# Query heads of an encoder layer turned two at a time, with the high and low parts of odd heads in exchanged rows

## The chip, the cores and the metric

The kernel runs on one core of a Trainium2 chip. A core has engines with queues of their own: PE (TensorE, matrix products; its weight loads are shown as PEld), DVE (VectorE), ACT (ScalarE), POOL (GpSimd) and SP (SyncE, which here only issues DMAs). Each works through its queue in order, and an instruction waits until the semaphores that it names have come. The metric is the time of one execution on the device in microseconds. A profile records one execution.

## The reference

One layer of a bidirectional encoder on two sequences of 512 tokens, width 1024: an RMS norm, one input projection, a window attention and a state-space branch, both gated and added, an output projection, and a squared-ReLU MLP. What matters here is the attention, with 16 query heads and 4 key heads of 64 channels, in blocks of 128 tokens:

```python
def windowed_attention(q, k, v, sink, bias, mask):
    ...
        s = jnp.einsum('nqkgd,njkd->nkgqj', qb, kw).astype(jnp.float32) * scale + bias
        s = jnp.where(mask[:, None, None], s, NEG_INF)
        sink_col = jnp.broadcast_to(sink_b, s.shape[:-1] + (1,))
        p = jax.nn.softmax(jnp.concatenate([s, sink_col], axis=-1), axis=-1)[..., :-1]
        o = jnp.einsum('nkgqj,njkd->nqkgd', p.astype(vs.dtype), vw)
...
    q = rms_norm(q.reshape(bsz, seq_len, N_HEADS, HEAD_DIM), q_gain)
    k = rms_norm(k.reshape(bsz, seq_len, N_KV_HEADS, HEAD_DIM), k_gain)
```

Each query block of 128 tokens sees its own block of keys and the two beside it.

## The kernel before

Every fp32 product is made of parts in the type fp32r: a high part (a rounded copy, written by ACT) and a low part (the rest, written by DVE). A product of two such operands takes three matmuls: high by high, high by low and low by high.

The program has these stages: norm and turn of x, input projections beside the state-space branch, a short stretch that projects the values and the first query tiles (up to about 459 us), the attention loop (to about 695 us), the gates and the output projection, and the MLP.

The attention loop goes over eight steps, one for each pair of key head `j` and sequence `sq`, and in each over four query blocks `qb`. The text calls one pass a unit, so a step is units 0 to 3. Units 0 and 3 have two key blocks (256 keys), units 1 and 2 three (384 keys). A unit works on three things at once, in an order written out by hand (lines 979 to 1073), which PE, ACT, DVE and POOL keep as it stands:

- `cur`, the unit itself: `scores` (L823, PE), `largest` (L827, DVE, adds the bias and takes the row's largest), `exp` (L833, ACT).
- `prev`, the unit before: `turn` (L839, PE, transposes the probabilities), `high` (L843, ACT), `low` (L848, DVE), `value` (L855, PE, product with the values), `lower_part` (L859, ACT) and `add` (L865, DVE).
- the query tile for the next step (class `Tile`): `project` (L772, PE), `square` (L778, ACT), `power` (L782, DVE, and two POOL instructions), `norm` (L789, DVE), and then, one unit later, `turn` (L794, PE), `high` (L799, ACT) and `low` (L802, DVE).

A step also turns the next keys in unit 0 (L754 on PE, L755 on ACT, L756 on DVE), and in unit 1 it sends its row sums to DRAM and fetches the factor `fac`, by which DVE multiplies the step before in unit 3 (L893). Weight pieces come in between (L730 on ACT, L731 on DVE).

The score product has 128 rows of contraction. For one head, the query operand `qa` holds the 64 channels of the high part in rows 0 to 63 and those of the low part in rows 64 to 127. The keys are copied twice before they are turned, so `kh` has the high part of the same 64 channels in both halves of its rows, and `kl` the low part. Two matmuls with `kh` and `kl` then give all four products of parts.

The changed methods have 32 tiles to work on: three before the loop (their `turn`, `high` and `low` stand among the products of the values), four in each of steps 0 to 6 and one in step 7. In unit 0 the tile belongs to the step itself, in the others to the next.

Of the kernel before, what the change touches and what calls it, by code (L numbers as in the profile page):

```python
# [12 lines left out]
F32 = mybir.dt.float32  # L13
F32R = mybir.dt.float32r
I32 = mybir.dt.int32
AF = mybir.ActivationFunctionType
ALU = mybir.AluOpType
AX = mybir.AxisListType

P = 128  # L20
# [7 lines left out]
CB = 256  # L28
N_HEADS = 16
N_KV = 4  # L30
G = 4
# [32 lines left out]
def hybrid_layer(ctx, tc, x, rel, onehot, w_qkv, w_ug, vectors, lam, coefs, w_glu, w_out, ln2,  # L64
                 w_up, w_down, out):
    nc = tc.nc
    V, S, PE, GP, SP = nc.vector, nc.scalar, nc.tensor, nc.gpsimd, nc.sync
# [12 lines left out]
    def acc():  # L80
        return ps_acc.tile([P, 512], F32, tag="acc", name="acc")
# [22 lines left out]
    ident = const.tile([P, P], F32, name="ident")  # L104
# [5 lines left out]
    bglu_sb, gain_q, gain_k, nsink = [vec[:, a:b] for a, b in ((0, 8), (8, 9), (9, 10), (10, 26))]  # L110
# [331 lines left out]
    with tc.tile_pool(name="hst", bufs=1) as hp:  # L442
        h = hp.tile([P, NCHUNK, 2, GROUPS, NSEQ], F32, name="h")
# [251 lines left out]
    with tc.tile_pool(name="att", bufs=2, reuse_waits="tile") as ap, tc.tile_pool(name="attc", bufs=1, reuse_waits="tile") as ac:  # L695
# [18 lines left out]
        weights, keys, queries, biases = {}, {}, {}, {}  # L714
# [44 lines left out]
        class Tile:  # L759
# [30 lines left out]

            def turn(self):
                self.pt = self.pt or acc()
                for h in range(G):
                    PE.transpose(self.pt[0:64, h * P:(h + 1) * P], self.qn[:, h], ident)  # L794

            def high(self):
                self.ptv = self.pt[0:64].rearrange("p (h t) -> p h t", h=G)
                self.dst = queries[self.key][:, :, self.t * P:(self.t + 1) * P]
                S.activation(self.dst[0:64], self.ptv, AF.Copy, scale=gain_q[0:64])  # L799

            def low(self):
                V.scalar_tensor_tensor(self.dst[64:128], self.ptv, gain_q[0:64], self.dst[0:64].bitcast(F32),  # L802
                                       op0=ALU.mult, op1=ALU.subtract)

        class Unit:

# [133 lines left out]
        rows = None  # L940
        for t in range(4):
# [9 lines left out]
            rows = new  # L951
# [21 lines left out]
        with tc.manual_schedule(engines={ET.PE, ET.Activation, ET.DVE, ET.Pool}):  # L973
            for i, (j, sq) in enumerate(steps):
# [4 lines left out]
                for qb in range(NB):  # L979
                    if 1 <= i < 5:  # L980
                        e, t = divmod((i - 1) * NB + qb, T)
# [89 lines left out]
                    owed, prev, rows = prev, cur, new  # L1071
# [36 lines left out]
    with tc.tile_pool(name="glu", bufs=1, reuse_waits="tile") as gpool, \  # L1108
# [40 lines left out]
        for u in range(2 * KT):  # L1149
            m, s = divmod(u, 2)  # L1150
# [151 lines left out]
    with tc.tile_pool(name="up", bufs=2, reuse_waits="tile") as fp:  # L1302
        turn = itertools.count()

        def parts(src):
            i = next(turn) % KT
            hi, lo = [q[:, i, :].rearrange("p (k n) -> p k n", k=4) for q in ring]
            S.copy(hi, src)  # L1308
            V.tensor_sub(lo, src, hi.bitcast(F32))  # L1309
            return hi, lo  # L1310
# [239 lines left out]
```

## Time and profile before

| what | value |
| --- | --- |
| runs shown | 1509.11, 1509.28, 1507.25 us; median 1509.11 |
| the profiled execution | 1509.57 us, of which the span of recorded work is 1507.8 us |
| granted TensorE clock, mean over the span | 0.993 |
| DMA, mean over the span | 166 GB/s |
| DVE busy in `low` of the query tiles (L802) | 23.8 us in 32 instructions |
| ACT busy in `high` of the query tiles (L799) | 21.5 us in 32 instructions |
| PE matmuls of the turns (L794) | 128 |

A line of the time line has the start in us from the span's start, the duration in us, engine, line and operation, what is written and read, the shape, and a count; in brackets stands how long the engine was idle before it and what ended that. Several PE instructions in a row are merged, and their matmuls overlap each other. A line of the groups has the count, then the busy time in us and the mean of one in ns, then the idle time before.

### The profile page before, as it was taken

What the parts mean: (1) busy time and instruction counts of PE and PEld (TensorE: products, weight loads), DVE (VectorE), ACT (ScalarE), POOL (GpSimd) and SP (SyncE); (2) the same over time, 40 slices, a digit from 0 to 9 for tenths busy, and PEclk for the clock granted to TensorE, in tenths of its full rate; (3) what the DMA queues carried; (4) which work ended last, traced back from release to release, by engine and by line L of the source; (5) the groups of instructions that cost most, each with busy time, mean ns of one, the idle gap of its engine ahead of it and who ended that gap; (6) DMA issues with size and microseconds to landing.
All of it is one profiled execution on the core that took longest, in us unless ns stands there. A gap on an engine that the chain in (4) does not pass through costs nothing. (4 is left out here: it accounts for less than half of the span.)

```text
span 1507.8 us, 22144 instructions
## 1 busy us (share of the span) xinstructions
PE 1452.1 (96%) x8074; PEld 1232.2 (82%) x8074; DVE 1116.3 (74%) x2015; ACT 763.4 (51%) x1362; POOL 192.4 (13%) x362
## 2 busy tenths in 40 slices
PE   6999999999999999997999989999999999999998
PEld 4788888888999998985787878888888888888787
DVE  7998859986647998886985478777777588575653
ACT  6777852235436787783343255544555443433332
POOL 3143341002232332220100000000000000000000
PEclk9999999999999999998999999999999999999999
DMA  4454469239731444373644234444443694454431
GB/s 173 140 168 168 164 211 344 98 111 352 279 103 36 149 138 142 111 257 110 224 164 170 94 103 173 154 153 154 154 154 126 251 361 135 154 181 154 126 122 61
DMA packets 102141, 249.69 MB, mean 166 GB/s; under 512 B 12266, under 2 KB 23786, under 8 KB 102032
## 3 DMA queue, kind: packets, MB, share of 16 engines
q1 hardware_dynamic: 58352, 135.88, 27.6%
q0 software_dynamic: 18048, 57.72, 11.1%
q10 hardware_dynamic: 25632, 54.67, 9.7%
q8 instruction: 64, 1.05, 0.3%
q14 instruction: 45, 0.37, 0.1%
HBM read 173.74 MB, written 90.21 MB: 175 GB/s over the span
## 5 line engine op out<-in xcount | busy, mean ns | idle before, releaser
L185 PE MATMUL acc<-act,c_hi 128*128 128x512 f32 x768 | 249.8, 400 | 1.0 <-DVE act L304 1.0
L117 PE MATMUL bank<-b_lo,a_hi 128*128 128x512 f32 x448 | 174.6, 390 | 1.3 <-DVE b_lo L1419 1.1
L118 PE MATMUL bank<-b_hi,a_lo 128*128 128x512 f32 x448 | 174.3, 389 | 0.0
L116 PE MATMUL bank<-b_hi,a_hi 128*128 128x512 f32 x448 | 173.5, 389 | 0.0
L185 PEld LDWEIGHTS acc<-act,c_hi 128*128 128x128 f32 x768 | 142.2, 189 | 29.2 <-DVE act L304 2.4
L185 PE MATMUL acc<-act,c_lo 128*128 128x512 f32 x384 | 152.5, 397 | 0.0
L1418 ACT CAST a_hi<-d_a 128x1024 fp32r<-128x1024 f32 x56 | 59.1, 1054 | 179.5 <-PE bank L117 176.1
L116 PE MATMUL bank<-act,act 128*128 128x512 f32 x368 | 144.3, 392 | 4.9 <-ACT act L1308 4.9
L117 PE MATMUL bank<-act,act 128*128 128x512 f32 x368 | 144.0, 391 | 0.0
L118 PE MATMUL bank<-act,act 128*128 128x512 f32 x368 | 143.9, 391 | 0.0
L1419 DVE TENSOR_TENSOR a_lo<-d_a,a_hi 128x1024 fp32r<-128x1024 f32 x56 | 68.5, 1223 | 100.0 <-ACT a_hi L1418 100.0
L772 PE MATMUL acc<-w_hi,act 128*128 128x256 f32 x512 | 116.1, 295 | 0.0
L117 PEld LDWEIGHTS bank<-b_lo,a_hi 128*128 128x128 f32 x448 | 84.1, 188 | 19.6 <-DVE b_lo L1419 2.3
L116 PEld LDWEIGHTS bank<-b_hi,a_hi 128*128 128x128 f32 x448 | 84.1, 188 | 17.6
L118 PEld LDWEIGHTS bank<-b_hi,a_lo 128*128 128x128 f32 x448 | 84.1, 188 | 17.4
L123 PE MATMUL acc<-act,gc_hi 128*128 128x512 f32 x256 | 83.9, 407 | 13.7 <-ACT ga L1133 10.7
L772 PEld LDWEIGHTS acc<-w_hi,act 128*128 128x128 f32 x512 | 86.9, 189 | 3.7
L116 PEld LDWEIGHTS bank<-act,act 128*128 128x128 f32 x368 | 69.6, 189 | 19.8 <-ACT act L1308 5.3
L185 PEld LDWEIGHTS acc<-act,c_lo 128*128 128x128 f32 x384 | 72.6, 189 | 13.8 <-DVE c_lo L176 0.5
L833 ACT ACTIVATE p<-p,nmx 128x257 f32<-128x257 f32 (+1 forms) x128 | 72.2, 564 | 22.7 <-DVE nmx L827 21.1
L118 PEld LDWEIGHTS bank<-act,act 128*128 128x128 f32 x368 | 69.6, 189 | 14.8 <-DVE act L1309 0.4
L117 PEld LDWEIGHTS bank<-act,act 128*128 128x128 f32 x368 | 69.6, 189 | 14.4
(328 smaller groups left out, 3426.5 us busy)
## 6 DMA issues: line engine op xcount, KB each, us to landing
d_a<-a_scr SPq DMA_DIRECT2D x56, 512.0 KB, 3.6
u_raw<-in_w_up_dram SPq DMA_DIRECT2D x32, 512.0 KB, 5.1
a_scr<-t ACTq DMA_DIRECT2D x64, 256.0 KB, 5.0
k<-in_w_down_dram SPq DMA_DIRECT2D x32, 512.0 KB, 6.0
c_raw<-in_w_ug_dram SPq DMA_DIRECT2D x48, 256.0 KB, 3.8
a_scr<-a ACTq DMA_DIRECT2D x46, 256.0 KB, 2.1
ct_scr<-ctab POOLq DMA_DIRECT2D x16, 576.0 KB, 3.9
ctab_in<-ct_scr POOLq DMA_DIRECT2D x16, 576.0 KB, 7.8
```

The costliest lines, as they stand in the source:

```text
L116: PE.matmul(ps, a[0], b[0], start=first, stop=False)
L117: PE.matmul(ps, a[0], b[1], start=False, stop=False)
L118: PE.matmul(ps, a[1], b[0], start=False, stop=last)
L123: PE.matmul(ps, w[wi][:, k, :], rows[yi], start=k + p == 0, stop=k == KT - 1 and p == 2)
L185: PE.matmul(ps, w[wi][:, k, :], hT[s][hi][:, k, :], start=n == 0, stop=n == 3 * KT - 1)
L772: PE.matmul(self.ps, hT[sq][act][:, k, col:col + P], w[:, k % 4, :], start=i == 0, stop=i == 3 * KT - 1)
L833: S.activation(p, p, AF.Exp, bias=self.nmx[:, h:h + 1], scale=-1.0, accum_out=self.sums[:, h, self.qb:self.qb + 1])
L1418: S.copy(hi, src)
L1419: V.tensor_sub(lo, src, hi.bitcast(F32))
```

## The change

In the four heads of a tile the first and third are even (e = 0), the second and fourth odd (e = 1). Before, each head was turned by itself: a 128x64 block becomes 64 rows of 128 tokens. Now two neighbouring heads are turned together: a 128x128 block becomes 128 rows, with the even head in rows 0 to 63 and the odd one in rows 64 to 127. Even heads keep their layout in `qa`. For odd heads the high part is written to rows 64 to 127, where it was turned to, and the low part to rows 0 to 63. As both halves of the key operands hold the same channels, the scores are the same sums.

`high` and `low` each work on one parity at a time, so each becomes two instructions of 64 rows and 256 columns where there was one of 64 rows and 512.

```diff
             def turn(self):
                 self.pt = self.pt or acc()
-                for h in range(G):
-                    PE.transpose(self.pt[0:64, h * P:(h + 1) * P], self.qn[:, h], ident)
+                for m in range(2):
+                    PE.transpose(self.pt[:, m * P:(m + 1) * P],
+                                 self.qn[:, 2 * m:2 * m + 2].rearrange("p e d -> p (e d)"), ident)
 
             def high(self):
-                self.ptv = self.pt[0:64].rearrange("p (h t) -> p h t", h=G)
-                self.dst = queries[self.key][:, :, self.t * P:(self.t + 1) * P]
-                S.activation(self.dst[0:64], self.ptv, AF.Copy, scale=gain_q[0:64])
+                self.ptv = self.pt[:, 0:CB].rearrange("p (m t) -> p m t", m=2)
+                self.dst = [queries[self.key][:, e::2, self.t * P:(self.t + 1) * P] for e in range(2)]
+                for dst, rows in zip(self.dst, (slice(0, 64), slice(64, 128))):
+                    S.activation(dst[rows], self.ptv[rows], AF.Copy, scale=gain_q[rows])
 
             def low(self):
-                V.scalar_tensor_tensor(self.dst[64:128], self.ptv, gain_q[0:64], self.dst[0:64].bitcast(F32),
-                                       op0=ALU.mult, op1=ALU.subtract)
+                for dst, rows, other in zip(self.dst, (slice(0, 64), slice(64, 128)), (slice(64, 128), slice(0, 64))):
+                    V.scalar_tensor_tensor(dst[other], self.ptv[rows], gain_q[rows], dst[rows].bitcast(F32),
+                                           op0=ALU.mult, op1=ALU.subtract)
```

On PE nothing but the turn changes. This is its first place, in the stretch before the loop, with the rows of before and of the change; `act` are the turned tokens, `qn` is the normed query tile, and `ident` the identity matrix.

```order
 L772 MATMUL acc<-w_lo,act_103 128x256
 L772 MATMUL acc<-w_hi,act_104 128x256
-L794 MATMUL acc<-ident,qn 64x128 x4
+L794 MATMUL acc<-ident,qn 128x128 x2
 L116 MATMUL acc<-w_hi,act_103 128x256
 L117 MATMUL acc<-w_lo,act_103 128x256
```

Four transposes with 64 output rows became two with 128, at the same place.

On DVE this is unit 3 of step 2 before, with the semaphores that each instruction waits for; `p` are the scores, `nmx` the row's largest, `tps` and `ph` the turned probabilities and their high part, `pl` their low part.

```order
L848 TENSOR_TENSOR pl<-tps,ph 128x512 [waits DVE_49,Activation_49]
L827 ISA p,nmx<-sps,bias,vec 128x256 [waits PE_49]
L827 ISA nmx 128x1
L802 SCALAR_TENSOR_TENSOR qa<-acc,vec,qa 64x4x128 [waits Activation_49]
L848 TENSOR_TENSOR pl<-tps,ph 128x512 [waits DVE_49,Activation_49]
L782 TENSOR_REDUCE ms<-sq 128x4 [waits Activation_49]
```

And the same place now, where three source lines more shift the numbers (L830 was L827, L851 was L848, L805 was L802):

```order
L851 TENSOR_TENSOR pl<-tps,ph 128x512 [waits DVE_49,Activation_49]
L830 ISA p,nmx<-sps,bias,vec 128x256 [waits PE_49]
L830 ISA nmx 128x1
L805 SCALAR_TENSOR_TENSOR qa<-acc,vec,qa 64x2x128 [waits PE_49,Activation_49]
L805 SCALAR_TENSOR_TENSOR qa<-acc,vec,qa 64x2x128
L851 TENSOR_TENSOR pl<-tps,ph 128x512 [waits DVE_49,Activation_49]
L782 TENSOR_REDUCE ms<-sq 128x4 [waits Activation_49]
```

The low part became two instructions, one behind the other; only the first has waits, on ACT and on PE.

On ACT, unit 3 of step 2 before; `vec` holds the gain, `ol` is the lower half of the value product.

```order
L833 ACTIVATE p,sm<-p,nmx 128x257 [waits DVE_49]
L799 ACTIVATE qa<-acc,vec 64x4x128 [waits PE_49]
L843 CAST ph<-tps 128x512 [waits PE_49,Activation_49]
L833 ACTIVATE p,sm<-p,nmx 128x257 [waits DVE_49]
L778 ACTIVATE sq<-acc 128x256 [waits PE_49]
```

And now (L836 was L833, L801 was L799, L846 was L843):

```order
L836 ACTIVATE p,sm<-p,nmx 128x257 [waits DVE_49]
L801 ACTIVATE qa<-acc,vec 64x2x128 [waits PE_49]
L801 ACTIVATE qa<-acc,vec 64x2x128
L846 CAST ph<-tps 128x512 [waits PE_49,Activation_49]
L836 ACTIVATE p,sm<-p,nmx 128x257 [waits DVE_49]
L778 ACTIVATE sq<-acc 128x256 [waits PE_49]
```

The high part became two instructions in a row, the second without a wait. Apart from the three steps of the tile the order on PE, ACT, DVE and POOL is the same. On SP one load of weights and one store of row sums change places in step 7.

## The prediction

> **What bounds the kernel now.** First the busy time of each engine, over the span and by stage.
>
> ```profile
> PE 1452.1 (96%) x8074; PEld 1232.2 (82%) x8074; DVE 1116.3 (74%) x2015; ACT 763.4 (51%) x1362; POOL 192.4 (13%) x362
> ...
> core 0: us, PE busy (x) PEld busy (x) DVE busy (x) ACT busy (x) POOL busy (x), PEclk, DMA share, GB/s
> 433.00:455.00 22.00, 22.00 (x187) 22.00 (x186) 6.85 (x14) 4.86 (x11) 4.50 (x8) 1.00 0.00 1
> 516.00:545.00 29.00, 28.03 (x209) 25.90 (x207) 26.23 (x67) 22.65 (x58) 9.71 (x17) 1.00 0.45 135
> ```
>
> PE leads the whole span, but the changed lines run only between 432 and 668 us, so the stage counts. In its first part (433 to 455 us) PE is busy all the time and DVE a third of it. In the attention loop (516 to 545 us is one step of four units, about 29 us) PE has 28.0 us, but DVE has 26.2 us too. The share does not say which of them sets the pace. The waits between 459 and 672 us and the time lines do.
>
> ```profile
> PEld po L855 <- DVE pl L848: 8.7, 20, 0.8
> ...
> 533.23 0.60 PE L794 MATMUL acc<-ident,qn 128*64 128x128 f32 x4
> 533.67 0.60 PE L839 MATMUL tps<-ident,p 128*128 128x128 f32 x4
> 536.91 0.50 PE L855 MATMUL po<-pl,va 128*128 128x512 f32 x1 [0.51 <-DVE pl L848]
> ...
> 521.44 0.75 DVE L756 SCALAR_TENSOR_TENSOR kl<-tps,vec,kh 128x512 fp32r<-128x512 f32 x1 [0.97 <-ACT kh L755]
> 522.22 0.74 DVE L802 SCALAR_TENSOR_TENSOR qa<-acc,vec,qa 64x512 fp32r<-64x512 f32 x1
> 523.09 0.42 DVE L782 TENSOR_REDUCE ms<-sq 128x4 f32<-128x256 f32 x1
> 529.79 0.42 DVE L782 TENSOR_REDUCE ms<-sq 128x4 f32<-128x256 f32 x1 [0.27 <-ACT sq L778]
> 534.15 0.68 DVE L848 TENSOR_TENSOR pl<-tps,ph 128x512 fp32r<-128x512 f32 x1
> 534.75 0.61 DVE L827 CUSTOM_DVE_ANT_0 p<-sps,bias,vec 128x384 f32<-128x384 f32 x1
> 535.39 0.74 DVE L802 SCALAR_TENSOR_TENSOR qa<-acc,vec,qa 64x512 fp32r<-64x512 f32 x1
> 536.17 0.69 DVE L848 TENSOR_TENSOR pl<-tps,ph 128x512 fp32r<-128x512 f32 x1
> 537.69 0.49 DVE L827 CUSTOM_DVE_ANT_0 p<-sps,bias,vec 128x256 f32<-128x256 f32 x1 [0.51 <-PE sps L823]
> 538.43 1.23 DVE L893 TENSOR_TENSOR ya<-ya,fac 128x1024 f32<-128x1024 f32 x1 [0.25 <-DMA fac<-rs_scr]
> 543.52 0.74 DVE L802 SCALAR_TENSOR_TENSOR qa<-acc,vec,qa 64x512 fp32r<-64x512 f32 x1 [0.24 <-ACT qa L799]
> 544.29 0.69 DVE L848 TENSOR_TENSOR pl<-tps,ph 128x512 fp32r<-128x512 f32 x1
> ...
> 520.71 0.69 ACT L755 ACTIVATE kh<-tps,vec 128x512 fp32r<-128x512 f32 x1 [0.61 <-PE tps L754]
> 521.30 0.67 ACT L799 ACTIVATE qa<-acc,vec 64x512 fp32r<-64x512 f32 x1
> 528.78 0.62 ACT L833 ACTIVATE p<-p,nmx 128x385 f32<-128x385 f32 x1 [0.30 <-DVE nmx L827]
> 542.31 0.51 ACT L833 ACTIVATE p<-p,nmx 128x257 f32<-128x257 f32 x1 [0.26 <-DVE nmx L827]
> 542.82 0.67 ACT L799 ACTIVATE qa<-acc,vec 64x512 fp32r<-64x512 f32 x1
> 543.39 0.57 ACT L843 CAST ph<-tps 128x512 fp32r<-128x512 f32 x1
> ```
>
> These are PE, DVE and ACT of step 2. The pace passes from engine to engine. Unit 0 runs at PE's pace: DVE waits 0.97 us at L756 for a chain that PE's key transposes release. In unit 1 DVE works on without a break from 523.09, and its one idle stretch, 0.27 us, stands behind the query step at 529.79. In unit 2 the last L848 of DVE (536.17) lies behind the query's L802 (535.39), and PE stands until it ends. In unit 3 the chain is L833, L799 on ACT, then L802 and L848 on DVE. So an instruction on DVE or ACT beside the query step is on the path in units 2 and 3, and one that PE saves is on it in unit 0 alone.
>
> Whether the end of the loop reaches the end of the program is seen behind it:
>
> ```profile
> 681.84 1.22 DVE L893 TENSOR_TENSOR ya<-ya,fac 128x1024 f32<-128x1024 f32 x1
> ...
> 702.10 1.23 DVE L893 TENSOR_TENSOR ya<-ya,fac 128x1024 f32<-128x1024 f32 x1 [6.95 <-DMA fac<-rs_scr]
> ```
>
> The last factor (702.10) comes back from DRAM after 6.95 us of waiting and all that follows hangs on it, so I take the rest as moved whole. The factor before it (681.84) is not waited for.
>
> **The change, part by part.** Prices first.
>
> ```profile
> L794 PE MATMUL acc<-ident,qn 128*64 128x128 f32 x128 | 19.3, 273 | 0.0
> L799 ACT ACTIVATE qa<-acc,vec 64x512 fp32r<-64x512 f32 x32 | 21.5, 673 | 0.8 <-PE acc L794 0.5
> L802 DVE SCALAR_TENSOR_TENSOR qa<-acc,vec,qa 64x512 fp32r<-64x512 f32 x32 | 23.8, 744 | 3.3 <-ACT qa L799 2.5
> L843 ACT CAST ph<-tps 128x512 fp32r<-128x512 f32 x80 | 46.1, 576 | 6.8 <-PE tps L839 6.2
> L710 ACT CAST va<-acc 128x256 fp32r<-128x256 f32 x8 | 3.0, 373 | 20.6 <-PE acc L118 20.6
> L848 DVE TENSOR_TENSOR pl<-tps,ph 128x512 fp32r<-128x512 f32 x80 | 54.9, 686 | 2.1 <-ACT ph L843 1.6
> L789 DVE TENSOR_TENSOR qn<-acc,rq 128x256 f32<-128x256 f32 x32 | 13.3, 414 | 5.9 <-POOL rq L785 5.9
> L335 DVE SCALAR_TENSOR_TENSOR ex_q<-ex_q,ex_r 128x64 f32<-128x64 f32 x10 | 2.3, 226 | 0.2
> ```
>
> PE, per tile of 32: four L794 hold the stream from 533.23 to 533.67, 0.11 each. Four L839, which load 128 columns where L794 loads 64, read 0.60 in the time line too, so a wider one should cost the same. Two fewer give **-0.22 us**; the other end is 0, if a transpose twice as wide took twice as long.
>
> ACT, per tile: one 64x512 becomes two 64x256. From L843 to L710, 256 columns fewer save 0.203 us, so a half is 0.673 - 0.203 = 0.47. The next ACT instruction starts 0.10 before the old one's end (543.39 against 542.82 + 0.67), so the pair ends after 0.37 + 0.47 = 0.84 where the one took 0.67: a = **+0.17 us**. Ends: 0 (only the columns count) and +0.27 (no overlap).
>
> DVE, per tile: one 64x512 becomes two 64x256. By L848 and L789 a half saves 0.272, giving 0.744 - 0.272 = 0.47; by L335, the same operation at 64 columns, (0.744 - 0.226) / 448 gives 0.45. The next instruction starts 0.03 to 0.04 after L802's end (536.17 against 536.13). The pair so takes 2 x 0.505 = 1.01 where the one took 0.78: d = **+0.23 us**. The upper end is +0.37, if a half saved only ACT's 0.203; the lower is +0.12, if a half let its successor in 0.08 early, as L848 does (534.75 against 534.15 + 0.68) and L802 does not. I take 0.23 because L802's own rows show no overlap.
>
> The Trainium skill, "VectorE: DVE Perf Modes", section "Two Vector instructions with no wait between them", holds an instruction back until the earlier ones have finished when its start quadrant of input or output differs from that used last; L802 reads the lower rows and writes the upper ones, and the trace agrees with its gap of 0.03 us. The second half then reads and writes the other way round, so both are held and d = 0.23; without the rule d would be 0.12.
>
> The wait between them: in the changed order the first DVE half waits for ACT and the second waits for nothing, though it reads what the second ACT half wrote. So the first waits for both ACT halves; the two pairs do not run side by side. Behind DVE's pair stand the next L848 and PE's last value product; behind ACT's pair the next L843 or L833. DMA queues, POOL and SP get nothing from the tile steps; one store and one load on SP change places in step 7, ahead of the factor at 681.84, and as DVE does not wait for that one I count nothing.
>
> The sum, with d = 0.23, a = 0.17.
> - Before the loop: three tiles, PE alone busy: 3 x -0.22 = -0.66.
> - Unit 0, steps 1 to 6: L756 starts 0.22 earlier at 521.22 and DVE is free 0.78 + 0.78 + 0.23 later, at 523.01 instead of L782's 523.09. ACT's pair ends at 521.08 + 0.84 = 521.92 and is covered. -0.08 each, -0.48.
> - Unit 1: L802 stretches by 0.23 into the 0.27 us before L782; ACT's L833 waits 0.30 for DVE, which covers a. 0. If that cover went, d would count here too, 1.4 us in six steps.
> - Unit 2: DVE is unbroken, d counts whole. Steps 1, 3, 6: 3 x 0.23. Steps 2 and 4 wait for the factor straight behind it (0.25 and 0.66), which covers d: 0. In step 5 L802 waits for ACT itself: a + d = 0.40. Together 1.09.
>
> ```profile
> 597.38 1.23 DVE L893 TENSOR_TENSOR ya<-ya,fac 128x1024 f32<-128x1024 f32 x1 [0.66 <-DMA fac<-rs_scr]
> 623.28 0.75 DVE L802 SCALAR_TENSOR_TENSOR qa<-acc,vec,qa 64x512 fp32r<-64x512 f32 x1 [0.21 <-ACT qa L799]
> 484.93 0.74 DVE L802 SCALAR_TENSOR_TENSOR qa<-acc,vec,qa 64x512 fp32r<-64x512 f32 x1
> 668.55 0.62 DVE L827 CUSTOM_DVE_ANT_0 p<-sps,bias,vec 128x384 f32<-128x384 f32 x1 [0.74 <-PE sps L823]
> ```
>
> - Unit 3, steps 1 to 6: the chain from 542.31 goes through both pairs: a + d = 0.40 each, 2.40.
> - Step 0: -0.22 (PE's pace at first), +0.23 in unit 2, and in unit 3 (484.93, no idle time before it) d with little of a, 0.28: +0.29.
> - Step 7 has one tile, and DVE waits for PE behind it (668.55): -0.22.
>
> The sum is -0.66 - 0.48 + 1.09 + 2.40 + 0.29 - 0.22 = **+2.4 us**. The profiled execution took 1509.57 (its span 1507.8 and 1.8 around it) and would take 1512.0; the median of the three runs is 1509.11, 0.5 lower, so the forecast is **1511.5**. With the lower ends (a = 0, d = 0.12) the same walk gives -0.8, with the upper ones +6.5.
>
> **The rivals.** 0.2% is 3.0 us, about what a measurement of this kernel can tell from no change.
> - PE sets the pace everywhere. For it: 28 of 29 us busy. Against it: DVE's waits for PE are short, and PE's waits at L855 stand in all steps. It would give 32 x -0.22 = -7.0: 1502.1.
> - The pairs cost more than their rows say. Place: unit 3, ACT to DVE, and unit 2. At d = 0.30 and a = 0.20 the walk gives +4.2: 1513.3. It decides from d = 0.26 on, a half of 0.52 us with its gap. For it: no row has this operation at 64x256. Against it: three slopes put the half at 0.45 to 0.47.
> - The first DVE half starts behind the first ACT half. In unit 3 it would start at 543.32, and L848 at 544.33 instead of 544.29: 0.04 in place of 0.40. The sum is about -0.2: 1509.0. Against it: the order of waits. The Trainium skill, "PSUM — Partial Sum Buffer", section "PSUM bank collisions raise a hardware error", has two engines collide only in one bank and one quadrant, and the halves read different ones, so by it nothing forbids this; no run here shows it.
> - The change does not save on PE, because a wider transpose takes 0.22: the terms -0.66, -0.22 (twice) go, and unit 0 adds 0.14 six times in place of its gain: +4.8, 1513.9. Against it: L839's 0.60.
>
> **How the numbers follow.** Chances: my walk 0.51 (of which 0.08 come out over +3.0), dearer pairs 0.27, halves side by side 0.10, PE everywhere 0.07, no saving 0.05. Faster by over 0.2%: 0.07. Slower: 0.08 + 0.27 + 0.05 = 0.40. Within: 0.43 + 0.10 = 0.53. The range goes from the lower ends (1509.11 - 0.8, and 0.3 for the spread of the runs), 1508.0, to 1515.0; it leaves out the PE rival and the top of the dear pairs.
>
> **What would show it.** In the changed profile: PE turns at 0.22 for two; ACT halves near 0.47, the second 0.37 behind the first; DVE halves near 0.47, 0.50 apart, the first never before the second ACT half ends; DVE's wait for ACT in unit 3 up from 0.24 to about 0.4; L782's 0.27 in unit 1 nearly gone; PE's waits at L855 longer. Steps 1 to 6 would each be 0.3 to 0.7 us longer, most at 0.55. Wrong would be: DVE halves over 0.50, a first half that starts early, or waits at L855 that vanish.

## The result, and the profile after it

The changed kernel takes 1516.69 us (median of 4 runs, 1515.52 to 1517.74) and the kernel before 1509.19 us (4 runs, 1507.25 to 1510.24). The ratio is 1.0051, with a 95% interval from 1.0037 to 1.0065: the change makes the kernel 5.6 to 9.8 us slower. The forecast was 2.4 us slower, with a range that ended at 1515.0. The direction was right, the size too small by a factor of three. The two profiled executions (1515.52 and 1509.57 us) differ by 5.95 us, less than the medians (7.5), so what is read from the profiles below explains these 5.95 us; the other 1.5 is not seen in them, and the runs of one kernel spread by 2 to 3 us.

Besides the lines named above, L858 was L855, L885 was L882 (a small copy on ACT) and L896 was L893. The page of the changed kernel (profiled execution 1515.52 us) says:

```profile
span 1513.4 us, 22103 instructions
...
PE 1450.7 (96%) x8010; PEld 1226.0 (81%) x8010; DVE 1123.6 (74%) x2047; ACT 773.6 (51%) x1394; POOL 192.1 (13%) x362
```

PE has 1.4 us less work, DVE 7.3 us and ACT 10.2 us more, and the span is 5.6 us longer. So PE stands still for 7.0 us more than before. The waits between 459 and 677 us say for what (us in total, times, longest):

```profile
PEld po L858 <- DVE pl L851: 16.9, 25, 1.1
...
PE po L858 <- DVE pl L851: 9.3, 14, 0.8
...
DVE qa L805 <- ACT qa L801: 4.8, 10, 0.6
...
DVE ms L782 <- ACT sq L778: 1.4, 7, 0.4
```

For DVE's low part of the weights the weight loads waited 8.7 us before and wait 16.9 now. DVE itself waits more for ACT's high part of the queries (2.5 before), and less at L782 (5.5 before), where it now comes later itself.

The two lines of the query step, all 64 instructions of each (min, median, max in ns; first and last start):

```profile
L801 ACT ACTIVATE qa<-acc,vec x64: 452/468/473, 432.2 to 672.0; 64x256 fp32r<-64x256 f32 x64
...
L805 DVE SCALAR_TENSOR_TENSOR qa<-acc,vec,qa x64: 476/483/490, 434.7 to 673.0; 64x256 fp32r<-64x256 f32 x64
```

A half takes 0.468 and 0.483 us, near the 0.47 that three slopes had given. The durations were not the error. The time line of step 2 shows what stands between the instructions. First the kernel before, in rows that were not shown yet:

```profile
528.13 0.60 DVE L827 CUSTOM_DVE_ANT_0 p<-sps,bias,vec 128x384 f32<-128x384 f32 x1
...
530.12 0.61 DVE L827 CUSTOM_DVE_ANT_0 p<-sps,bias,vec 128x384 f32<-128x384 f32 x1
...
529.30 0.19 ACT L833 ACTIVATION_READ_ACCUMULATOR p<-p,nmx 128x1 f32 x1
529.39 0.36 ACT L778 ACTIVATE sq<-acc 128x256 f32<-128x256 f32 x1
...
523.42 0.61 DVE L827 CUSTOM_DVE_ANT_0 p<-sps,bias,vec 128x384 f32<-128x384 f32 x1
```

And the same step of the changed kernel, DVE, then ACT:

```profile
521.68 0.75 DVE L756 SCALAR_TENSOR_TENSOR kl<-tps,vec,kh 128x512 fp32r<-128x512 f32 x1 [0.76 <-ACT kh L755]
522.52 0.98 DVE L805 SCALAR_TENSOR_TENSOR qa<-acc,vec,qa 64x256 fp32r<-64x256 f32 x2
523.55 0.42 DVE L782 TENSOR_REDUCE ms<-sq 128x4 f32<-128x256 f32 x1
524.01 0.62 DVE L830 CUSTOM_DVE_ANT_0 p<-sps,bias,vec 128x384 f32<-128x384 f32 x1
...
528.72 0.61 DVE L830 CUSTOM_DVE_ANT_0 p<-sps,bias,vec 128x384 f32<-128x384 f32 x1
...
530.52 0.42 DVE L782 TENSOR_REDUCE ms<-sq 128x4 f32<-128x256 f32 x1 [0.17 <-ACT sq L778]
530.97 0.62 DVE L830 CUSTOM_DVE_ANT_0 p<-sps,bias,vec 128x384 f32<-128x384 f32 x1
...
536.25 0.98 DVE L805 SCALAR_TENSOR_TENSOR qa<-acc,vec,qa 64x256 fp32r<-64x256 f32 x2
537.27 0.69 DVE L851 TENSOR_TENSOR pl<-tps,ph 128x512 fp32r<-128x512 f32 x1
...
544.55 0.98 DVE L805 SCALAR_TENSOR_TENSOR qa<-acc,vec,qa 64x256 fp32r<-64x256 f32 x2 [0.51 <-ACT qa L801]
...
528.24 0.24 ACT L885 COPY row<-tps 16x128 f32<-16x128 f32 x1
528.39 0.94 ACT L801 ACTIVATE qa<-acc,vec 64x256 fp32r<-64x256 f32 x2
529.37 0.62 ACT L836 ACTIVATE p<-p,nmx 128x385 f32<-128x385 f32 x1
529.89 0.19 ACT L836 ACTIVATION_READ_ACCUMULATOR p<-p,nmx 128x1 f32 x1
530.10 0.38 ACT L778 ACTIVATE sq<-acc 128x256 f32<-128x256 f32 x1
...
543.58 0.94 ACT L801 ACTIVATE qa<-acc,vec 64x256 fp32r<-64x256 f32 x2
544.54 0.59 ACT L846 CAST ph<-tps 128x512 fp32r<-128x512 f32 x1
```

Three things are to be seen.

- **DVE's pair** takes 0.98 and its successor starts 0.03 behind it (536.25 to 537.27: 1.02 where L802 to L848 was 0.78). That is d = 0.24.
- **ACT's pair** takes 0.94: its halves do not overlap, and the next ACT instruction starts 0.96 behind the pair's start (543.58 to 544.54), where it was 0.57 (542.82 to 543.39). DVE, which started 0.70 behind L799 in unit 3, starts 0.97 behind L801 (544.55). So a = 0.27 for DVE, and 0.39 for ACT's next instruction. DVE's first half waits for both ACT halves, though they read different rows.
- **Instructions behind the pairs, which the change does not touch,** start later than they did. L830 starts 0.46 and 0.45 behind L782 (523.55 to 524.01, 530.52 to 530.97), where it was 0.33. ACT's `sq` starts 0.21 behind the accumulator's read (529.89 to 530.10), where it was 0.09.

To see where the steps grew, take PE's last value product (L855, now L858) in units 2 and 3 of each step as marks in both time lines. Between the marks the loop grew by (us; the forecast's terms beside it):

| step | units 0 to 2, forecast | measured | unit 3, forecast | measured |
|---|---|---|---|---|
| 1 | 0.15 | 0.63 | 0.40 | 0.49 |
| 2 | -0.08 | 0.63 | 0.40 | 0.17 |
| 3 | 0.15 | 0.64 | 0.40 | 0.50 |
| 4 | -0.08 | 0.63 | 0.40 | -0.26 |
| 5 | 0.32 | 1.00 | 0.40 | 0.50 |
| 6 | 0.15 | 0.63 | 0.40 | 0.51 |
| sum | 0.61 | 4.16 | 2.40 | 1.91 |

In steps 2 and 4 the wait for the factor takes something back. The forecast had put that into unit 2; the factor stands behind PE's mark, so the measurement shows it in unit 3. The growth reaches the end whole. This is the last factor in the time line of the changed kernel, 5.40 us later than before:

```profile
707.50 1.23 DVE L896 TENSOR_TENSOR ya<-ya,fac 128x1024 f32<-128x1024 f32 x1 [7.18 <-DMA fac<-rs_scr]
```

### The profile page after: what moved, and what is told of

Read it like the earlier page. It is cut to its first block, busy times and chain, and to the rows that moved or that the text cites. A ratio compares the mean times of both kernels' runs of the same rounds, so it can differ in the third digit from the quotient of the medians.

```text
span 1513.4 us, 22103 instructions
## 1 busy us (share of the span) xinstructions
PE 1450.7 (96%) x8010; PEld 1226.0 (81%) x8010; DVE 1123.6 (74%) x2047; ACT 773.6 (51%) x1394; POOL 192.1 (13%) x362
## 4 chain that ended last, share of the span: by engine, by line
PE 76%; DVE 9%; issue 5%; ACT 4%; DMA 3%; POOL 1%; ACTq 0%; SPq 0%; DVEq 0%; POOLq 0%
PE acc L185 14%; PE bank L118 13%; PE bank L117 13%; PE bank L116 13%; PE acc L123 5%; PE acc L117 2%; PE acc L118 2%; PE acc L116 2%; DVE pl L851 2%; PE acc L772 2%; PE sps L547 2%; PE po L858 1%; PE sps L826 1%; DVE p L830 1%; DVE ya L868 1%
## 5 line engine op out<-in xcount | busy, mean ns | idle before, releaser
L836 ACT ACTIVATE p<-p,nmx 128x257 f32<-128x257 f32 (+1 forms) x128 | 72.3, 565 | 22.5 <-DVE nmx L830 21.1
```

Of the source, the lines that this page charges most:

```text
L836: S.activation(p, p, AF.Exp, bias=self.nmx[:, h:h + 1], scale=-1.0, accum_out=self.sums[:, h, self.qb:self.qb + 1])
```

## The experiments

Two theories were set against each other. **H**: the costs come from the exchange of rows, because an instruction that starts in other rows of PSUM than the one before it on its engine is held until that one has ended; this makes the pairs longer and holds what stands behind them. **S**: the costs come from splitting one instruction into two. A time below is the difference that the ratio gives, times 1509; its 95% interval stands behind it. The change itself is counted by its medians, 7.5 (its ratio gives 7.7).

### One part of the change alone

The turn alone, with one instruction each on ACT and DVE (the edit of `turn` is that of the change):

```diff
...
 def high(self):
-    self.ptv = self.pt[0:64].rearrange("p (h t) -> p h t", h=G)
-    self.dst = queries[...]
+    pt = self.pt[0:64, 0:CB].rearrange("p (m t) -> p m t", m=2)
+    self.ptv = pt[:, None].to_broadcast([64, 2, 2, P])
+    self.dst = queries[...].rearrange("p (e m) t -> p e m t", e=2)
     S.activation(self.dst[0:64], self.ptv, AF.Copy, scale=gain_q[0:64])
```

> The two wide turns of the change, with one ACT and one DVE instruction per tile as before, both reading the lower 64 rows. Heads 0 and 2 of a tile stand in for all four (heads 0, 1, 2, 3 get the queries of 0, 2, 0, 2), so the scores of the others are not computed from their own queries. Theory 1 (PE saves 0.22 us a tile, but it is on the path only before the loop and in unit 0): about -2.6 us against the kernel before. Rival (PE sets the pace everywhere): -7. Rival (a wide turn saves nothing): 0.

Measured: -2.7 us (-4.4 to -1.1). So the turn saves what the forecast had it save, and PE does not set the pace everywhere.

The split alone, with the rows and turns of before:

```diff
-S.activation(self.dst[0:64], self.ptv, ...)
+for hs in (slice(0, 2), slice(2, 4)):
+    S.activation(self.dst[0:64, hs], self.ptv[:, hs], ...)
...
-V.scalar_tensor_tensor(self.dst[64:128], self.ptv, ...)
+for hs in (slice(0, 2), slice(2, 4)):
+    V.scalar_tensor_tensor(self.dst[64:128, hs], self.ptv[:, hs], ...)
```

> The kernel before with its four turns and its rows, but two ACT and two DVE instructions per tile, heads 0 and 1 and heads 2 and 3. Theory H: ACT's pair takes 0.84 (+0.17), DVE's pair 0.91 (+0.13), nothing else gets longer; units 0 and 1 cover it, unit 2 gives 0.13 and unit 3 0.30 a step: about +2.8 us against the kernel before. Theory S: ACT's pair 0.94 and DVE's 1.02 as in the change, about +5.7.

Measured: +3.5 us (2.3 to 4.8). H's 2.8 lies inside the interval, S's 5.7 outside. Unit 3 of step 2 in its time line (here L800 and L804 are the pairs):

```profile
542.84 0.81 ACT L800 ACTIVATE qa<-acc,vec 64x256 fp32r<-64x256 f32 x2
...
543.68 0.87 DVE L804 SCALAR_TENSOR_TENSOR qa<-acc,vec,qa 64x256 fp32r<-64x256 f32 x2 [0.38 <-ACT qa L800]
```

The pairs take 0.81 and 0.87, not 0.94 and 0.98. The first DVE half reads only what the first ACT half wrote, and yet it starts 0.84 behind the pair's start, behind both. So in the order as written the halves do not run side by side even where no data ties them. Both engines read the same rows here, so for halves in different rows only the changed kernel speaks, where DVE's first half starts behind both ACT halves too (0.97).

The change with both pairs in the lower rows of PSUM (split and turn without the exchange):

```diff
-for dst, rows in zip(self.dst, (slice(0, 64), slice(64, 128))):
+for dst, rows in zip(self.dst, (slice(0, 64), slice(0, 64))):
...
-for dst, rows, other in zip(self.dst, (slice(0, 64), slice(64, 128)), (slice(64, 128), slice(0, 64))):
+for dst, rows, other in zip(self.dst, (slice(0, 64), slice(0, 64)), (slice(64, 128), slice(64, 128))):
```

> The change with one difference: both pairs of heads are read from the lower rows of PSUM, the high part goes to rows 0 to 63 and the low part to rows 64 to 127 for all heads. Wide turns, two ACT and two DVE instructions stay. The odd heads get the queries of the even ones. Theory H (moving between lower and upper rows makes an instruction on ACT and DVE wait for the end of the one before it; the loss is mostly this): ACT's pair takes 0.84 and its second half starts 0.37 behind the first, DVE's pair 0.91, the DVE scores behind L782 start 0.33 behind it; about +0.5 us against the kernel before. Theory S (the second instruction of a pair costs what it costs, whatever the rows): as the change, +6.

Measured: +0.5 us (-0.9 to +2.0). The exchange of rows is what makes the change slow: without it 7 of its 7.5 us are gone. Units 1 and 2 of step 2 in its time line:

```profile
532.82 0.42 DVE L782 TENSOR_REDUCE ms<-sq 128x4 f32<-128x256 f32 x1
533.16 0.61 DVE L830 CUSTOM_DVE_ANT_0 p<-sps,bias,vec 128x384 f32<-128x384 f32 x1
...
538.43 0.87 DVE L805 SCALAR_TENSOR_TENSOR qa<-acc,vec,qa 64x256 fp32r<-64x256 f32 x2
539.33 0.69 DVE L851 TENSOR_TENSOR pl<-tps,ph 128x512 fp32r<-128x512 f32 x1
...
537.31 0.81 ACT L801 ACTIVATE qa<-acc,vec 64x256 fp32r<-64x256 f32 x2
538.02 0.57 ACT L846 CAST ph<-tps 128x512 fp32r<-128x512 f32 x1
```

DVE's pair hands over after 0.90 instead of 1.02, ACT's after 0.71 instead of 0.96, and L830 is back at 0.34 behind L782. The parts add up: turn -2.7, split +3.5, together +0.8, measured +0.5; with the exchange +7.5.

The exchange without the split, that is the turn alone, read from the upper rows:

```diff
-    pt = self.pt[0:64, 0:CB]...
+    pt = self.pt[64:128, 0:CB]...
...
-    S.activation(self.dst[0:64], self.ptv, AF.Copy, scale=gain_q[0:64])
+    S.activation(self.dst[64:128], self.ptv, AF.Copy, scale=gain_q[64:128])
...
-    V.scalar_tensor_tensor(self.dst[64:128], self.ptv, gain_q[0:64], self.dst[0:64].bitcast(F32),
+    V.scalar_tensor_tensor(self.dst[0:64], self.ptv, gain_q[64:128], self.dst[64:128].bitcast(F32),
```

> As e1_turn_alone, but the one ACT and the one DVE instruction of a tile read the upper 64 rows of PSUM, write the high part to rows 64 to 127 and the low part to rows 0 to 63: the exchange of rows without a second instruction. All heads get the queries of odd ones. Theory H (an instruction whose rows differ from those used last waits for the end of the one before it, on ACT and on DVE): ACT's instruction starts 0.10 later, the scores behind L782 on DVE start 0.45 behind it, `square` behind `exp` 0.21 behind its read of the sum; about 0.36 us a step, in all about +1 us against the kernel before, 3.5 more than e1. Rival (only a pair with different rows pays): as e1, -2.7.

Measured: +1.1 us (-0.3 to +2.4), 3.8 more than the turn alone. There is no second instruction here, so this is the exchange by itself, as H expects and S does not. Unit 1 of step 2 in its time line (here L829 is the row maximum):

```profile
528.53 0.42 DVE L782 TENSOR_REDUCE ms<-sq 128x4 f32<-128x256 f32 x1 [0.40 <-ACT sq L778]
528.98 0.62 DVE L829 CUSTOM_DVE_ANT_0 p<-sps,bias,vec 128x384 f32<-128x384 f32 x1
```

L829 starts 0.45 behind L782, as late as in the change, and `sq` starts 0.21 behind the accumulator's read (527.90 to 528.11).

### Which engine, and which instruction

The change, with DVE's second instruction reading the lower rows as its first:

```diff
-for dst, rows, other in zip(...):
-    V.scalar_tensor_tensor(dst[other], self.ptv[rows], gain_q[rows], dst[rows].bitcast(F32),
+for dst, other in zip(self.dst, (slice(64, 128), slice(0, 64))):
+    V.scalar_tensor_tensor(dst[other], self.ptv[0:64], gain_q[0:64], self.dst[0][0:64].bitcast(F32),
```

> The change with DVE's second instruction on the lower rows of PSUM (it takes the even heads' values and writes rows 0 to 63 of the odd heads, so the low part of odd heads is not theirs); ACT's pair as in the change. ACT's pair takes 0.94 and DVE's 0.91. Theory H with both engines at fault: about 2 us over e2, +2.5 against the kernel before. If ACT's pair is all of it: +7. If DVE's pair is all of it: +0.5.

Measured: +4.1 us (2.1 to 5.9). The expectation of 2.5 lies inside the interval, "all on ACT" (7) and "all on DVE" (0.5) lie outside. DVE in units 1 and 2 of step 2:

```profile
528.06 0.42 DVE L782 TENSOR_REDUCE ms<-sq 128x4 f32<-128x256 f32 x1 [0.18 <-ACT sq L778]
528.40 0.61 DVE L830 CUSTOM_DVE_ANT_0 p<-sps,bias,vec 128x384 f32<-128x384 f32 x1
...
533.67 0.97 DVE L805 SCALAR_TENSOR_TENSOR qa<-acc,vec,qa 64x256 fp32r<-64x256 f32 x2
534.57 0.67 DVE L851 TENSOR_TENSOR pl<-tps,ph 128x512 fp32r<-128x512 f32 x1
```

DVE's pair still takes 0.97, not the 0.91 expected, though both halves read the same rows. What still differs between them is the rows that they write (0 to 63 and 64 to 127 of `qa`, in SBUF). So an exchange of written rows holds an instruction too, and H, which names PSUM alone, is too narrow for DVE. But behind the pair L851 starts after 0.90 (1.02 in the change) and L830 starts 0.34 behind L782 (0.45). So DVE's exchanged reads cost the hold behind the pair, 0.11 or 0.12 in each of the four units of a step, and without them 3.4 of the 7.5 us are gone: six steps of 0.46 would be 2.8, and with intervals of about 2 us to either side the two agree. What is left, 3.6 us over the kernel with the rows kept, is by the profiles mostly ACT's: DVE hands over after 0.90 and L830 starts 0.34 behind L782 in both, while ACT's pair takes 0.94 here and 0.81 there, and `sq` starts 0.21 behind the accumulator's read here (527.44 to 527.65) and 0.09 there (532.33 to 532.42).

DVE's instruction alone split, rows and ACT as before:

```diff
-V.scalar_tensor_tensor(self.dst[64:128], self.ptv, ...)
+for hs in (slice(0, 2), slice(2, 4)):
+    V.scalar_tensor_tensor(self.dst[64:128, hs], self.ptv[:, hs], ...)
```

> The kernel before with VectorE's instruction on the turned tile split in two by heads (rows and turns as before). Theory (the split's 3.5 us come from both engines: DVE's pair longer by about 0.13 us in units 2 and 3, where L848 sets PE, and ACT's by 0.15): 1.5 us more than before, so that ACT's split is worth the other 2. Rival, all on DVE: 3.5 us more. Rival, all on ACT: 0.

Measured: +2.7 us (1.1 to 4.4). That rules out 0 and leaves 1.5 and 3.5 both open. In the two profiles the stretch from the first to the last L782 is 233.9 us before (428.1 to 662.0) and 235.2 here (428.4 to 663.6), 1.3 more, and 236.2 (427.1 to 663.3) with both split, 2.3 more. That speaks for 1.5 and a part for ACT, but each is a single execution. The same stretch is 239.8 in the change (427.2 to 667.0), 233.5 with the rows kept (431.2 to 664.7) and 236.1 with DVE reading the lower rows (426.0 to 662.1): the exchange shows in the loop itself as it does in the times.

The odd heads first, so that the instruction in the lower rows stands last and what is behind it is not held:

```diff
-for dst, rows in zip(...):
+for dst, rows in list(zip(...))[::-1]:
```

> The change with the odd heads ahead of the even ones in both pairs, so that the last read of PSUM on ACT and DVE is from the lower rows. Theory H: the instruction behind ACT's pair starts 0.10 before its end again, and the first scores on DVE in units 0 and 1 start 0.33 behind L782 in place of 0.46; about 0.38 us less in each of steps 1 to 6, that is 2.3 us less than the change. Theory S: as the change.

Measured: +7.2 us (5.1 to 9.2), as slow as the change: a miss. Unit 1 of step 2 in its time line:

```profile
531.92 0.24 ACT L885 COPY row<-tps 16x128 f32<-16x128 f32 x1
532.18 0.95 ACT L801 ACTIVATE qa<-acc,vec 64x256 fp32r<-64x256 f32 x2
533.04 0.62 ACT L836 ACTIVATE p<-p,nmx 128x385 f32<-128x385 f32 x1
...
533.17 0.98 DVE L805 SCALAR_TENSOR_TENSOR qa<-acc,vec,qa 64x256 fp32r<-64x256 f32 x2 [0.16 <-ACT qa L801]
534.18 0.42 DVE L782 TENSOR_REDUCE ms<-sq 128x4 f32<-128x256 f32 x1
534.52 0.61 DVE L830 CUSTOM_DVE_ANT_0 p<-sps,bias,vec 128x384 f32<-128x384 f32 x1
```

What was expected behind the pairs came: L830 starts 0.34 behind L782 again, and L836 0.86 behind the pair's start instead of 0.98. But now the first half is held: L801 starts 0.26 behind the start of L885, where it was 0.15 in the change (528.24 to 528.39). DVE waits for it (0.16, where it waited for nothing here in the change). The expectation had overlooked that there are two holds per pair in either order: one between the halves, and one where the odd half meets its neighbour. Reversing moves the second; it does not take it away.

### Another place for the query step

If only the work in front of the last L848 of a unit cost time, the step could be moved behind it. First both `high` and `low`, in the kernel before and in the change:

```diff
-if rows:
-    rows.high()
-    rows.low()
 if n3 > 2:
     prev.high(2)
...
 if n3 > 2:
     prev.low(2)
+if rows:
+    rows.high()
+    rows.low()
```

> The kernel before with the query tile's high and low part moved behind the probabilities' last high and low part in every unit (the loop's order alone; the queries are wanted a step later). Theory (the query tile is on the path in units 2 and 3 only because it stands ahead of L848 on DVE): L848 and PE's last value product come up to 0.75 us earlier in unit 2 and about 0.3 in unit 3, about -5 us in all (-3 to -9). Rival (DVE is full, what is moved back delays the next unit by as much): 0.

> The change with the same move. Theory: the longer pairs lie behind the path and the wide turns' gain stays, so this is no slower than e7 and up to 2 us faster. Rival (DVE is full): the pairs cost the same 7 us over e7.

Measured: +5.3 us (3.3 to 7.1) in the kernel before and +21.0 us (18.9 to 23.1) in the change, two misses. The waits of the kernel before with the step moved, between 459 and 677 us:

```profile
ACT p L833 <- DVE nmx L827: 39.0, 78, 1.8
DVE qa L802 <- ACT qa L799: 21.1, 29, 1.4
```

L799 now stands behind an exponential that waits for DVE's row maximum, and L802 waits for L799: DVE to ACT to DVE, with L782 and the next unit queued behind. DVE waits 21.1 us for ACT there, where it was 2.5. In the change this move costs 13.5 us beyond its own 7.5. There DVE waits 28.9 us for ACT's pair, and PE's score products wait 20.0 us for DVE's row maxima, where it was 4.9 in the kernel before with the step moved: the longer pairs now stand on a chain on which PE waits.

Then DVE's part alone moved, ACT's left in its place:

```diff
 if rows:
     rows.high()
-    rows.low()
...
 if n3 > 2:
     prev.low(2)
+if rows:
+    rows.low()
```

> The kernel before, with only VectorE's instruction on the turned tile (L802) moved behind the low part of the weights (L848); ScalarE's L799 stays where it is. Theory (in units 2 and 3 the end of L848 sets PE, as the trace of before shows at L855): in unit 2 of step 2 ACT's ph is done by 535.4 and DVE is free at 535.4, so L848 starts about 0.75 us earlier, and PE's wait of 0.8 us at L855 nearly goes; with about 0.5 us in four steps of unit 2 and 0.3 us in six of unit 3, some 4 us less than before. Rival (every unit is bound by one chain through both engines, as in the run in which both instructions were moved): L782, which stands behind L802, and with it the next unit come no earlier, PE waits at another place, and the time is that of before or more (0 to +5 us).

> The change, with only VectorE's pair moved behind the low part of the weights; ScalarE's pair stays. Theory (of the change's 7.5 us about 3 to 4 are DVE's pair in front of L851 in units 2 and 3, the rest is ACT's pair and the held instructions in units 0 and 1): the first part goes and the gain of the same move on the kernel before comes on top, so some 7 us less than the change, within 3 us of before. Rival (the pairs lie on a chain through both engines wherever they stand): as slow as the change or slower, +7 us and more.

> The wide turn alone (one instruction on each engine, lower rows; heads 0 and 2 stand for all four, the odd heads aren't computed) with VectorE's instruction moved behind the low part of the weights. Theory: the two gains add, the turn's 2.7 us and the move's 4, so about 6.7 us less than before. Rival: the move gains nothing, and the time is that of the wide turn alone, 2.7 us less than before, or more.

Measured: -2.6 us (-4.5 to -0.6) in the kernel before, +7.1 us (4.5 to 9.5) in the change, and -7.2 us (-9.7 to -4.7) with the wide turn alone. The first and the third agree with the theory (-4 and -6.7 lie inside their intervals), the second is a miss, and its rival holds. Unit 3 of step 2, first L848 in the kernel before with `low` moved, then the change with `low` moved:

```profile
542.90 0.69 DVE L848 TENSOR_TENSOR pl<-tps,ph 128x512 fp32r<-128x512 f32 x1 [0.71 <-ACT ph L843]
...
542.01 0.94 ACT L801 ACTIVATE qa<-acc,vec 64x256 fp32r<-64x256 f32 x2
542.97 0.59 ACT L846 CAST ph<-tps 128x512 fp32r<-128x512 f32 x1
...
543.59 0.69 DVE L851 TENSOR_TENSOR pl<-tps,ph 128x512 fp32r<-128x512 f32 x1 [1.12 <-ACT ph L846]
544.31 0.98 DVE L805 SCALAR_TENSOR_TENSOR qa<-acc,vec,qa 64x256 fp32r<-64x256 f32 x2
545.33 0.42 DVE L782 TENSOR_REDUCE ms<-sq 128x4 f32<-128x256 f32 x1
```

DVE's pair is out of the way, but L851 now waits 1.12 us for ACT's `ph`, which stands behind ACT's pair; with the same move in the kernel before L848 waits 0.71. DVE's pair then delays L782 instead (545.33, 1.02 behind the pair's start), and the row maximum behind L782 is now held in this unit as well (0.45, 545.33 to 545.78). So one of the two engines is late in either place that was tried for DVE's part; how the 9.7 us between the two kernels divide among these holds was not measured.

So the kernel before with only `rows.low()` moved, at 1505.94 us against 1509.01 (ratio 0.9983, interval 0.9970 to 0.9996), is the fastest version found that computes all of it.

## Why the prediction was too small, point by point

- **PE's term held.** The turn alone gave -2.7 us, about what the expectation had worked out from 0.22 per tile.
- **d held.** 0.24 against 0.23. The Trainium skill's rule that the prediction weighed here, "VectorE: DVE Perf Modes", section "Two Vector instructions with no wait between them", agrees: with the rows kept the pair handed over after 0.90, which is d = 0.12, as the prediction said for the case without a hold. It agrees for the output too: in the run in which the halves differ only in the rows that they write, the pair was held (0.97).
- **Unit 1 is the step that failed** ("L802 stretches by 0.23 into the 0.27 us before L782; ACT's L833 waits 0.30 for DVE, which covers a. 0."), and unit 0 with it. Both covers did hold: ACT's exponential starts 0.65 behind the start of DVE's row maximum before and after (528.13 to 528.78, 528.72 to 529.37). What the prediction did not count is that the next instructions are held too. In unit 1 `sq` starts 0.73 behind the exponential instead of 0.61, and so L782 starts 1.80 behind the row maximum instead of 1.66: +0.14. L830 then starts 0.45 behind L782 instead of 0.33: +0.12. Together 0.26 per step where the forecast had 0.
- **Unit 0**: L756 to L782 took 1.65 and takes 1.87, where the forecast comes to 1.79 (0.78 + 0.78 + 0.23), because ACT's pair is not wholly covered (L805 starts 0.84 behind L756, L802 started 0.78); PE's saving pays for it (L756 waits 0.76 where it waited 0.97), which left -0.01 where the forecast had -0.08. But L830 behind L782 is held: +0.13. With unit 2's 0.24 the three units add 0.62 per step, and the table has 0.63. In step 5 DVE waits for ACT in units 1 and 2, so that a counts there as well: 1.00.
- **The same rule was read for the pair alone.** The prediction used it between the two halves. Applied further, to the next instruction that reads PSUM, it gives the late L830. The prediction had the row that prices such a loss: an unheld successor starts 0.08 us before L848's end.
- **a was mis-sized** in unit 3: 0.17 against 0.27, the upper end given, because ACT's halves do not overlap. Unit 3 so grows by 0.50 where nothing covers it, not by 0.40.
- **The rivals.** "PE everywhere" and "no saving" fall by the turn alone. "Halves side by side" falls for the order as written, by the changed kernel's own time line (0.97). With the parities in two PSUM banks, or with the instructions written alternately, it wasn't tried. "Dearer pairs" came true for ACT's pair; but the larger part of the miss in the profile is what stands behind the pairs in units 0 and 1: 0.13 + 0.14 + 0.12 = 0.39 us in each step, 2.3 in steps 1 to 6 of the 3.1 by which their sum (6.07) passed the forecast's (3.01). The rest is unit 0's 0.07, a in unit 3 and in step 5, less what the factor's wait took back.
- **Covers.** The forecast was right that the factor's wait covers steps 2 and 4. It covered more than d: against the 0.50 of the other steps, 0.33 and 0.76.

For DVE a run shows what the hold behind the pair costs (3.4 us by the run without DVE's exchanged reads, 2.8 by its time line). For ACT the division between a longer pair and the late `sq` is read from the profile alone: the reversal, which was to show it, moved one hold instead of removing it.

## What to carry to other kernels

Before an instruction is moved to other partitions, look at its neighbours on the engine, not at its own duration: what is lost is the overlap of 0.1 us with the instruction in front and with the next one behind that reads the same memory. A wait that covers an instruction does not cover its successors. Where two engines pass work to and fro, try to move only the half that delays the other engine: moving DVE's part alone gained 2.6 us, moving both parts lost 5.3.

## What the runs showed of the hardware

In these runs DVE and ACT both lose the overlap with the instruction in front when the rows change. On DVE this was seen for the rows read (L830 0.45 instead of 0.34 behind L782) and for the rows written (a pair of 0.97 instead of 0.87). On ACT only both together were tried. With both halves in the lower rows of PSUM ACT's pair took 0.81 us and the next instruction started 0.71 behind its start; with the second half in the upper rows it took 0.94 and the next started at 0.96; and `sq`, which is the next to read PSUM, with two instructions between, was late by 0.12 as well (0.21 instead of 0.09 behind the accumulator's read). The two kernels differ in the rows alone. Whether ACT's reads or its writes do it no run shows.
